# Group softmax: one exponential per tile without the maximum, sums on VectorE, and one test of all sums at the end

## The chip, the core and the metric

The kernel runs on one core of one Trainium2 chip. The core has engines that run beside one another, each with its own list of instructions: VectorE (DVE in the profile), ScalarE (ACT), GpSimd (POOL), TensorE (PE, which this kernel does not use before the change) and SyncE (SP), which issues transfers. They tell one another by semaphores when something is done. Sixteen DMA engines move data between the memory outside (HBM) and the core's own memory (SBUF), in which a tile lies as 128 partitions by some number of elements. A second on-chip memory, PSUM, is used by the changed kernel for small results.

The metric is the device time in microseconds of one execution. Lower is better.

## The reference

```python
def reference(x):                      # x: 4 x 4096 x 4352, float32, normal numbers
    B, N, D = x.shape
    G = 8
    Dg = D // G                        # 544
    x_g = x.reshape(B, N, G, Dg)
    x_g = x_g - x_g.max(axis=-1, keepdims=True)
    exp = np.exp(x_g)
    out = exp / exp.sum(axis=-1, keepdims=True)
    return out.reshape(B, N, D).astype(np.float32)
```

Each row of 4352 numbers is eight groups of 544, and each group gets a softmax of its own. Input and output are 285.21 MB each.

## The kernel before

The 16,384 rows are cut into 64 tiles (`nt`) of 128 partitions with two rows each (`R`), so a tile is 128 x 8704 elements and holds 16 groups per partition (`RG`). There are six buffers (`NT`, `bufs`), and a tile is worked in place in its buffer: tile t lies in buffer t % 6. The order on every engine is written out by hand, with semaphores.

- SP loads the tiles in order (L105). From tile 6 on it first waits until the store of the tile that had the buffer before has landed (`stored`). The last tile is loaded in two halves, one row of each partition at a time (L108), each with a semaphore of its own. Then SP issues the stores of the last two tiles (L113), each behind a wait until that tile is scaled.
- VectorE takes, for each tile, the negated maximum of each group (`vector_max`, L62), and later the reciprocal of the sums (L72) and one multiply of the whole tile by it (L75), both in `vector_scale`. The maximum of the next tile stands ahead of the reciprocal of this one. The list `parts` has 65 entries: 63 whole tiles and the two halves of the last.
- ScalarE takes, for each group, one exponential with the negated maximum as the bias, which also adds up the group's sum (`scalar_exp`, L86): 16 per tile. Its program has a loop around six tiles (L129), and the semaphore `max_done` is counted down once in each turn.
- GpSimd issues the stores of tiles 0 to 61 (L118), each behind a wait until the tile is scaled. At the end it waits until all stores have landed, those of SP too, and then the closing barrier of the block lets the other engines go on (L47).

The steps of the change and of the prediction touch `vector_max`, `scalar_exp` and `vector_scale`, the semaphores between them, and what the engines do after their last part. The loads and the stores, with their queues and their waits, are the same lines in both kernels.

Of the kernel before, what the change touches and what calls it, by code (L numbers as in the profile page):

```python
# [1 line left out]

# [4 lines left out]


@with_exitstack
def kernel(  # L10
    ctx: ExitStack,
    tc: tile.TileContext,
    x: bass.AP,
    out: bass.AP,
):
    nc = tc.nc
    G = 8
    P = 128
    R = 2
    NT = 6  # L20
    RG = R * G
    xf = x.flatten_outer_dims()
    of = out.flatten_outer_dims()
    N, D = xf.shape
    Dg = D // G
    nt = N // (P * R)
    LAST = 2
    FIRST = 2
    turns = (nt - 1 - FIRST) // NT
    f32 = mybir.dt.float32  # L30
    X = mybir.AxisListType.X
    Exp = mybir.ActivationFunctionType.Exp
    xt = xf.rearrange("(t p r) d -> t p (r d)", p=P, r=R)
    ot = of.rearrange("(t p r) d -> t p (r d)", p=P, r=R)

    landed = [tc.alloc_semaphore(f"landed{b}") for b in range(NT)]
    stored = [tc.alloc_semaphore(f"stored{b}") for b in range(NT)]
    last_landed = tc.alloc_semaphore("last_landed")
    last_stored = tc.alloc_semaphore("last_stored")


    max_done = tc.alloc_semaphore("max_done")
    exp_done = tc.alloc_semaphore("exp_done")
    rec_done = tc.alloc_semaphore("rec_done")
    scaled = tc.alloc_semaphore("scaled")

    ctx.enter_context(tc.tile_critical(  # L47
        sync_engine=mybir.EngineType.Pool, no_gpsimd_drain=True))
    bufs = [ctx.enter_context(nc.sbuf_tensor(f"xt{b}", [P, R * D], f32)) for b in range(NT)]
    mx = ctx.enter_context(nc.sbuf_tensor("mx", [P, NT, RG], f32))  # L50
    sm = ctx.enter_context(nc.sbuf_tensor("sm", [P, NT, RG], f32))
    rs = ctx.enter_context(nc.sbuf_tensor("rs", [P, NT, RG], f32))

    parts = [(t, slice(0, RG)) for t in range(nt - 1)]
    parts += [(nt - 1, slice(r * G, (r + 1) * G)) for r in range(R)]

    def groups(t, g):
        return bufs[t % NT][:, :].rearrange("p (g d) -> p g d", d=Dg)[:, g, :]

    def vector_max(n):  # L60
        t, g = parts[n]
        i = nc.vector.reduce_max(  # L62
            out=mx[:, t % NT, g], in_=groups(t, g), axis=X, negate=True)
        if g.start == 0:
            i.wait_op(landed[t % NT], 16 * (t // NT + 1), "sem-ge")
        else:
            i.wait_op(last_landed, 16, "sem-ge")
        i.then_inc(max_done, 1)

    def vector_scale(n):  # L70
        t, g = parts[n]
        nc.vector.reciprocal(out=rs[:, t % NT, g], in_=sm[:, t % NT, g]).wait_op(  # L72
            exp_done, n + 1, "sem-ge").then_inc(rec_done, 1)
        xg = groups(t, g)
        nc.vector.tensor_tensor(  # L75
            out=xg,
            in0=xg,
            in1=rs[:, t % NT, g].unsqueeze(2).to_broadcast([P, g.stop - g.start, Dg]),
            op=mybir.AluOpType.mult,
        ).wait_op(rec_done, n + 1, "sem-ge").then_inc(scaled, 1)  # L80

    def scalar_exp(n, count):
        t, gs = parts[n]
        xg = groups(t, gs)
        for g in range(gs.start, gs.stop):
            i = nc.scalar.activation(  # L86
                out=xg[:, g - gs.start, :],
                in_=xg[:, g - gs.start, :],
                func=Exp,
                bias=mx[:, t % NT, g:g + 1],  # L90
                scale=1.0,
                accum_out=sm[:, t % NT, g:g + 1],
            )
            if g == gs.start:
                i.wait_op(max_done, count, "sem-ge")
        i.then_inc(exp_done, 1)

    for t in range(nt):  # L100
        if t >= NT:
            nc.sync.wait_ge(stored[t % NT], 16 * (t // NT))
        tile_in = bufs[t % NT]
        if t < nt - 1:
            nc.sync.dma_start(out=tile_in[:, :], in_=xt[t]).then_inc(landed[t % NT], 16)  # L105
        else:
            for r in range(R):
                nc.sync.dma_start(  # L108
                    out=tile_in[:, r * D:(r + 1) * D], in_=xt[t, :, r * D:(r + 1) * D],
                ).then_inc(landed[t % NT] if r < R - 1 else last_landed, 16)  # L110
    for t in range(nt - LAST, nt):
        nc.sync.wait_ge(scaled, t + 1 if t < nt - 1 else len(parts))
        nc.sync.dma_start(out=ot[t], in_=bufs[t % NT][:, :]).then_inc(last_stored, 16)  # L113


    for t in range(nt - LAST):
        nc.gpsimd.wait_ge(scaled, t + 1)
        nc.gpsimd.dma_start(out=ot[t], in_=bufs[t % NT][:, :]).then_inc(stored[t % NT], 16)  # L118
    for t in range(nt - NT, nt - LAST):
        nc.gpsimd.wait_ge(stored[t % NT], 16 * (t // NT + 1))  # L120
    nc.gpsimd.drain()
    nc.gpsimd.wait_ge(last_stored, 16 * LAST)

    nc.scalar.preload_act_table(Exp)  # L124

    for n in range(FIRST):
        scalar_exp(n, n + 1)
    nc.scalar.sem_inc(max_done, -FIRST)
    with nc.scalar.Fori(0, turns):  # L129
        for k in range(NT):  # L130
            scalar_exp(FIRST + k, k + 1)
        nc.scalar.sem_inc(max_done, -NT)
    for k, n in enumerate(range(FIRST + turns * NT, len(parts))):
        scalar_exp(n, k + 1)


    vector_max(0)
    for n in range(len(parts)):
        if n + 1 < len(parts):
            vector_max(n + 1)  # L140
        vector_scale(n)


# [1 line left out]
_INS = ['x']  # L145
_OUTS = [((4, 4096, 4352), 'float32')]


# [23 lines left out]
```

## Time and profile before

| what | value |
|---|---|
| median of four runs | 1326.47 us (1326.45 to 1326.55) |
| the profiled execution, its own time | 1327.41 us |
| its span, first to last event of the profile | 1325.6 us |
| VectorE busy | 1190.0 us (90%) |
| ScalarE busy | 757.4 us (57%) |
| GpSimd busy | 33.3 us (3%) |
| moved | 570.48 MB, mean 430 GB/s over the span |
| load of a whole tile, issue to landing, median | 31.1 us |
| store from GpSimd, issue to landing, median | 52.8 us |

An engine's busy time is the sum of its instructions' times, and its share is taken of the span. The span is a little shorter than the execution's own time, since something lies around it. A line of a group names the source line, the engine, the operation, what is written and read with shapes, how often, then the busy time, the mean time of one in ns, and the engine's idle time just ahead of these instructions with what ended most of it. Two of the waits that the trace lists, in all, times and longest: VectorE's maximum waited 110.5 us in 51 waits for loads, and GpSimd's stores waited 1243.2 us in 62 waits for VectorE's multiply.

### The profile page before, as it was taken

The page shows a single profiled execution, that of the slowest core. Times are in us where ns is not written, and L with a number is a line of the kernel's source. Part 1 is how long each engine was busy: PE and PEld are TensorE (multiplying, and loading weights), DVE is VectorE, ACT ScalarE, POOL GpSimd, SP SyncE. Part 2 cuts the span into 40 slices and gives each one's busy share as a digit, 9 for nine tenths or more (in the row PEclk, how much of TensorE's full clock was granted, in tenths as well). Part 3 has the DMA queues.
Part 4 walks back from the last instruction along what each step waited for, and adds up shares of the span by engine and source line. Part 5 has one row for each costly group of instructions (what it writes and reads, how often), then busy time and mean ns, then how long its engine had stood idle before and what let it go on. Part 6 is the DMA issues. An engine that isn't in the chain of part 4 may idle for free.

```text
span 1325.6 us, 2465 instructions
## 1 busy us (share of the span) xinstructions
DVE 1190.0 (90%) x195; ACT 757.4 (57%) x2049; POOL 33.3 (3%) x66
## 2 busy tenths in 40 slices
DVE  5999999998989889899898898988989889898893
ACT  3765566547456465564655646547456474564651
POOL 0000000000000000000000000000000000000000
DMA  9999999999999999999999999999999999999998
GB/s 403 420 436 431 432 433 436 430 435 431 435 436 432 434 430 436 433 434 432 434 435 432 435 430 435 435 434 430 434 436 432 434 431 435 436 431 433 430 438 358
DMA packets 18582, 570.48 MB, mean 430 GB/s; under 512 B 2064, under 2 KB 2064, under 8 KB 2064
## 3 DMA queue, kind: packets, MB, share of 16 engines
q1 hardware_dynamic: 9648, 294.13, 51.5%
q0 software_dynamic: 8928, 276.30, 48.3%
q14 instruction: 6, 0.05, 0.0%
HBM read 285.21 MB, written 285.21 MB: 430 GB/s over the span
## 4 chain that ended last, share of the span: by engine, by line
another core or an unknown queue 69%; DVE 20%; DMA 7%; ACT 1%; SPq 1%; issue 0%; POOLq 0%
DVE xt L75 10%; DVE mx L62 10%; DMA out_dram<-xt 4%; DMA xt<-in_x_dram 3%; ACT xt L86 1%; SPq L105 1%; DVE rs L72 0%; SPq L167 0%; POOLq L47 0%; POOLq L156 0%
## 5 line engine op out<-in xcount | busy, mean ns | idle before, releaser
L86 ACT ACTIVATE xt<-xt,mx 128x544 f32<-128x544 f32 x1024 | 750.1, 734 | 542.2 <-DVE mx L62 542.2
L62 DVE TENSOR_REDUCE mx<-xt 128x16 f32<-128x8704 f32 (+1 forms) x65 | 590.1, 9079 | 110.5 <-DMA xt<-in_x_dram 110.5
L75 DVE TENSOR_TENSOR xt<-xt,rs 128x8704 f32<-128x8704 f32 (+1 forms) x65 | 590.6, 9085 | 2.2
L86 ACT ACTIVATION_READ_ACCUMULATOR xt<-xt,mx 128x1 f32 x1024 | 191.5, 187 | 0.0
L118 POOL DMA_DIRECT2D out_dram<-xt x62 | 33.1, 533 | 1243.2 <-DVE xt L75 1243.2
L72 DVE RECIPROCAL rs<-sm 128x16 f32<-128x16 f32 (+1 forms) x65 | 15.7, 241 | 2.8 <-ACT xt L86 2.8
L124 ACT ACT_TABLE_LOAD x1 | 1.3, 1283 | 0.9 <-PEq L156 0.9
L156 POOL MEMSET const-float32-0.0<- 128x1 f32 x1 | 0.1, 98 | 0.2 <-issue 0.2
L156 POOL MEMSET const-bfloat16-1.0<- 128x1 bf16 x1 | 0.1, 102 | 0.0
L156 POOL MEMSET const-float32-1.0<- 128x1 f32 x1 | 0.1, 98 | 0.0
L156 POOL MEMSET const-uint8-127<- 128x1 uint8 x1 | 0.1, 98 | 0.0
## 6 DMA issues: line engine op xcount, KB each, us to landing
xt<-in_x_dram SPq DMA_DIRECT2D x63, 4352.0 KB, 31.1
out_dram<-xt POOLq DMA_DIRECT2D x62, 4352.0 KB, 52.8
out_dram<-xt SPq DMA_DIRECT2D x2, 4352.0 KB, 21.5
xt<-in_x_dram SPq DMA_DIRECT2D x2, 2176.0 KB, 33.4
```

The lines of the kernel that those rows point to most:

```text
L62: i = nc.vector.reduce_max(out=mx[:, t % NT, g], in_=groups(t, g), axis=X, negate=True)
L72: nc.vector.reciprocal(out=rs[:, t % NT, g], in_=sm[:, t % NT, g]).wait_op(exp_done, n + 1, "sem-ge").then_inc(rec_done, 1)
L75: nc.vector.tensor_tensor(out=xg, in0=xg, in1=rs[:, t % NT, g].unsqueeze(2).to_broadcast([P, g.stop - g.start, Dg]), op=mybir.AluOpType.mu ...
L86: i = nc.scalar.activation(out=xg[:, g - gs.start, :], in_=xg[:, g - gs.start, :], func=Exp, bias=mx[:, t % NT, g:g + 1], scale=1.0, accum ...
L105: nc.sync.dma_start(out=tile_in[:, :], in_=xt[t]).then_inc(landed[t % NT], 16)
L118: nc.gpsimd.dma_start(out=ot[t], in_=bufs[t % NT][:, :]).then_inc(stored[t % NT], 16)
L124: nc.scalar.preload_act_table(Exp)
L156: nc = _bacc.Bacc("TRN2", target_bir_lowering=False, num_devices=1)
```

## The change

Without the subtraction of the maximum, exp(x) / sum(exp(x)) has the same value as long as the sums stay within the range of the numbers. The changed kernel uses that form for every tile. It leaves out `vector_max`; `scalar_exp` is one exponential of a whole part, with no bias and no accumulation, that waits for the load itself; ScalarE's loop is gone. `vector_scale` first takes the sums of the groups with a reduction on VectorE and writes them into PSUM, where the sums of all 64 tiles stay. Reciprocal and multiply are as before, with a wait of the reciprocal for the sums.

After the last multiply, `judge` takes maximum and minimum of all sums, marks those above 1e30 or below 1e-6, adds the marks over the partitions with a matmul of one column of ones, and stores a verdict. SP, ScalarE and VectorE load the verdict into a register and compare it. If it is above 0, they go through a loop over all tiles that computes the softmax with the maximum again, one tile at a time, and stores it over the first result. With the inputs of the reference this loop is not entered.

```diff
@@ -25,11 +25,11 @@
     Dg = D // G
     nt = N // (P * R)
     LAST = 2
-    FIRST = 2
-    turns = (nt - 1 - FIRST) // NT
+    LOW, HIGH = 1e-6, 1e30
     f32 = mybir.dt.float32
     X = mybir.AxisListType.X
     Exp = mybir.ActivationFunctionType.Exp
+    op = mybir.AluOpType
     xt = xf.rearrange("(t p r) d -> t p (r d)", p=P, r=R)
     ot = of.rearrange("(t p r) d -> t p (r d)", p=P, r=R)
 
@@ -37,65 +37,86 @@
     stored = [tc.alloc_semaphore(f"stored{b}") for b in range(NT)]
     last_landed = tc.alloc_semaphore("last_landed")
     last_stored = tc.alloc_semaphore("last_stored")
-
-
-    max_done = tc.alloc_semaphore("max_done")
     exp_done = tc.alloc_semaphore("exp_done")
+    sum_done = tc.alloc_semaphore("sum_done")
     rec_done = tc.alloc_semaphore("rec_done")
     scaled = tc.alloc_semaphore("scaled")
+    tested = tc.alloc_semaphore("tested")
+    counted = tc.alloc_semaphore("counted")
+    judged = tc.alloc_semaphore("judged")
+    again = {k: tc.alloc_semaphore(f"again_{k}") for k in ("in", "max", "exp", "rec", "out", "end")}
 
     ctx.enter_context(tc.tile_critical(
         sync_engine=mybir.EngineType.Pool, no_gpsimd_drain=True))
     bufs = [ctx.enter_context(nc.sbuf_tensor(f"xt{b}", [P, R * D], f32)) for b in range(NT)]
-    mx = ctx.enter_context(nc.sbuf_tensor("mx", [P, NT, RG], f32))
-    sm = ctx.enter_context(nc.sbuf_tensor("sm", [P, NT, RG], f32))
     rs = ctx.enter_context(nc.sbuf_tensor("rs", [P, NT, RG], f32))
+    mx = ctx.enter_context(nc.sbuf_tensor("mx", [P, RG], f32))
+    sm = ctx.enter_context(nc.sbuf_tensor("sm", [P, RG], f32))
+    one = ctx.enter_context(nc.sbuf_tensor("one", [P, 1], f32))
+    extreme = ctx.enter_context(nc.sbuf_tensor("extreme", [P, 4], f32))
+    outside = ctx.enter_context(nc.sbuf_tensor("outside", [P, 4], f32))
+    count = ctx.enter_context(nc.sbuf_tensor("count", [1, 1], f32))
+    verdict = ctx.enter_context(nc.sbuf_tensor("verdict", [1, 1], mybir.dt.int32))
+    half = nt // 2
+    sums = [ctx.enter_context(nc.psum_tensor(f"sums{h}", [P, half, RG], f32)) for h in range(2)]
+    found = ctx.enter_context(nc.psum_tensor("found", [1, 4], f32))
 
     parts = [(t, slice(0, RG)) for t in range(nt - 1)]
     parts += [(nt - 1, slice(r * G, (r + 1) * G)) for r in range(R)]
 
+    def grouped(b):
+        return bufs[b][:, :].rearrange("p (g d) -> p g d", d=Dg)
+
     def groups(t, g):
-        return bufs[t % NT][:, :].rearrange("p (g d) -> p g d", d=Dg)[:, g, :]
-
-    def vector_max(n):
+        return grouped(t % NT)[:, g, :]
+
+    def scalar_exp(n):
         t, g = parts[n]
-        i = nc.vector.reduce_max(
-            out=mx[:, t % NT, g], in_=groups(t, g), axis=X, negate=True)
+        i = nc.scalar.activation(out=groups(t, g), in_=groups(t, g), func=Exp, scale=1.0)
         if g.start == 0:
             i.wait_op(landed[t % NT], 16 * (t // NT + 1), "sem-ge")
         else:
             i.wait_op(last_landed, 16, "sem-ge")
-        i.then_inc(max_done, 1)
+        i.then_inc(exp_done, 1)
 
     def vector_scale(n):
         t, g = parts[n]
-        nc.vector.reciprocal(out=rs[:, t % NT, g], in_=sm[:, t % NT, g]).wait_op(
-            exp_done, n + 1, "sem-ge").then_inc(rec_done, 1)
+        s = sums[t // half][:, t % half, g]
+        nc.vector.reduce_sum(out=s, in_=groups(t, g), axis=X).wait_op(
+            exp_done, n + 1, "sem-ge").then_inc(sum_done, 1)
+        nc.vector.reciprocal(out=rs[:, t % NT, g], in_=s).wait_op(
+            sum_done, n + 1, "sem-ge").then_inc(rec_done, 1)
         xg = groups(t, g)
         nc.vector.tensor_tensor(
             out=xg,
             in0=xg,
             in1=rs[:, t % NT, g].unsqueeze(2).to_broadcast([P, g.stop - g.start, Dg]),
-            op=mybir.AluOpType.mult,
+            op=op.mult,
         ).wait_op(rec_done, n + 1, "sem-ge").then_inc(scaled, 1)
 
-    def scalar_exp(n, count):
-        t, gs = parts[n]
-        xg = groups(t, gs)
-        for g in range(gs.start, gs.stop):
-            i = nc.scalar.activation(
-                out=xg[:, g - gs.start, :],
-                in_=xg[:, g - gs.start, :],
-                func=Exp,
-                bias=mx[:, t % NT, g:g + 1],
-                scale=1.0,
-                accum_out=sm[:, t % NT, g:g + 1],
-            )
-            if g == gs.start:
-                i.wait_op(max_done, count, "sem-ge")
-        i.then_inc(exp_done, 1)
-
-
+    def judge():
+        nc.vector.memset(one[:, :], 1.0).then_inc(tested, 1)
+        flat = [s[:, :, :].rearrange("p t g -> p (t g)") for s in sums]
+        for h in range(2):
+            nc.vector.tensor_reduce(
+                out=extreme[:, h:h + 1], in_=flat[h], axis=X, op=op.max).then_inc(tested, 1)
+            nc.vector.tensor_reduce(
+                out=extreme[:, 2 + h:3 + h], in_=flat[h], axis=X, op=op.min).then_inc(tested, 1)
+        nc.vector.wait_ge(tested, 5)
+        nc.vector.tensor_scalar(
+            out=outside[:, 0:2], in0=extreme[:, 0:2], scalar1=HIGH, scalar2=None,
+            op0=op.is_gt).then_inc(tested, 1)
+        nc.vector.tensor_scalar(
+            out=outside[:, 2:4], in0=extreme[:, 2:4], scalar1=LOW, scalar2=None,
+            op0=op.is_lt).then_inc(tested, 1)
+        nc.tensor.wait_ge(tested, 7)
+        nc.tensor.matmul(
+            out=found[:, :], lhsT=one[:, :], rhs=outside[:, :],
+            start=True, stop=True).then_inc(counted, 1)
+        nc.vector.wait_ge(counted, 1)
+        nc.vector.reduce_sum(out=count[:, :], in_=found[:, :], axis=X).then_inc(tested, 1)
+        nc.vector.wait_ge(tested, 8)
+        nc.vector.tensor_copy(out=verdict[:, :], in_=count[:, :]).then_inc(judged, 1)
 
     for t in range(nt):
         if t >= NT:
@@ -112,7 +133,6 @@
         nc.sync.wait_ge(scaled, t + 1 if t < nt - 1 else len(parts))
         nc.sync.dma_start(out=ot[t], in_=bufs[t % NT][:, :]).then_inc(last_stored, 16)
 
-
     for t in range(nt - LAST):
         nc.gpsimd.wait_ge(scaled, t + 1)
         nc.gpsimd.dma_start(out=ot[t], in_=bufs[t % NT][:, :]).then_inc(stored[t % NT], 16)
@@ -122,23 +142,52 @@
     nc.gpsimd.wait_ge(last_stored, 16 * LAST)
 
     nc.scalar.preload_act_table(Exp)
-
-    for n in range(FIRST):
-        scalar_exp(n, n + 1)
-    nc.scalar.sem_inc(max_done, -FIRST)
-    with nc.scalar.Fori(0, turns):
-        for k in range(NT):
-            scalar_exp(FIRST + k, k + 1)
-        nc.scalar.sem_inc(max_done, -NT)
-    for k, n in enumerate(range(FIRST + turns * NT, len(parts))):
-        scalar_exp(n, k + 1)
-
-
-    vector_max(0)
     for n in range(len(parts)):
-        if n + 1 < len(parts):
-            vector_max(n + 1)
+        scalar_exp(n)
+
+    for n in range(len(parts)):
         vector_scale(n)
+    judge()
+
+    ET = mybir.EngineType
+    regs = nc.alloc_registers("verdict", [ET.SP, ET.Activation, ET.DVE])
+    for e, reg in zip((nc.sync, nc.scalar, nc.vector), regs):
+        e.reg_load(reg, verdict[0:1, 0:1]).wait_op(judged, 1, "sem-ge")
+    with nc.If_cmp(regs, 0, "IS_GT"):
+        for t in range(nt - NT, nt - LAST):
+            nc.sync.wait_ge(stored[t % NT], 16 * (t // NT + 1))
+        nc.sync.wait_ge(last_stored, 16 * LAST)
+        with nc.Fori(0, nt, engines=[ET.SP, ET.Activation, ET.DVE]) as t:
+            nc.sync.dma_start(out=bufs[0][:, :], in_=xt[bass.ds(t, 1)].rearrange("t p f -> (t p) f")).then_inc(
+                again["in"], 16)
+            nc.sync.wait_ge(again["out"], 1)
+            nc.sync.sem_inc(again["out"], -1)
+            nc.sync.dma_start(out=ot[bass.ds(t, 1)].rearrange("t p f -> (t p) f"), in_=bufs[0][:, :]).then_inc(
+                again["end"], 16)
+            nc.sync.wait_ge(again["end"], 16)
+            nc.sync.sem_inc(again["end"], -16)
+
+            nc.scalar.wait_ge(again["max"], 1)
+            nc.scalar.sem_inc(again["max"], -1)
+            for g in range(RG):
+                i = nc.scalar.activation(
+                    out=grouped(0)[:, g, :], in_=grouped(0)[:, g, :], func=Exp,
+                    bias=mx[:, g:g + 1], scale=1.0, accum_out=sm[:, g:g + 1])
+            i.then_inc(again["exp"], 1)
+
+            nc.vector.wait_ge(again["in"], 16)
+            nc.vector.sem_inc(again["in"], -16)
+            nc.vector.reduce_max(
+                out=mx[:, :], in_=grouped(0), axis=X, negate=True).then_inc(again["max"], 1)
+            nc.vector.wait_ge(again["exp"], 1)
+            nc.vector.sem_inc(again["exp"], -1)
+            nc.vector.reciprocal(out=rs[:, 0, :], in_=sm[:, :]).then_inc(again["rec"], 1)
+            nc.vector.wait_ge(again["rec"], 1)
+            nc.vector.sem_inc(again["rec"], -1)
+            nc.vector.tensor_tensor(
+                out=grouped(0), in0=grouped(0),
+                in1=rs[:, 0, :].unsqueeze(2).to_broadcast([P, RG, Dg]),
+                op=op.mult).then_inc(again["out"], 1)
 
 
 # ---- launch: one core; inputs and outputs as the reference has them ----
```

## The prediction, made before the changed kernel ran

> **What bounds the kernel now.** I read the busy shares first, then the chain of waits and SP's own waits, then the end of the span in windows.
>
> ```profile
> DVE 1190.0 (90%) x195; ACT 757.4 (57%) x2049; POOL 33.3 (3%) x66
> ...
> DMA  9999999999999999999999999999999999999998
> ...
> q1 hardware_dynamic: 9648, 294.13, 51.5%
> q0 software_dynamic: 8928, 276.30, 48.3%
> ```
>
> VectorE is busy 90% of the span, but the DMA row is at nine tenths or more in every slice except the last, and the two data queues together fill 99.8% of the span's engine time. So the bytes set the time: one 34,816-byte packet takes 1288 ns in the trace's DMA records in steady state, loads and stores alike, and the packets' time averaged over the 16 DMA engines is 1321.1 us. The first data packet starts at 2.3 us and the last one ends at 1324.2: there is 0.8 us of slack in 1322.
>
> The chain of waits shows the steady state, one load issue after another, 20.6 us apart, each held by a store that frees its buffer (the page can't name the store and calls it unknown; SP's own waits, below, name it):
>
> ```profile
> 1205.61 0.33 SPq L105
> 1205.94 20.27 another core or an unknown queue
> 1226.21 0.02 issue
> 1226.23 30.96 DMA xt<-in_x_dram
> ```
>
> ```profile
> SPq L105 <- DMA out_dram<-xt: 1203.1, 57, 67.6
> SPq L113 <- DVE xt L75: 57.3, 2, 42.1
> SPq L47 <- POOLq L47: 18.7, 1, 18.7
> ```
>
> The last row matters later: after its last store SP has nothing to do for 18.7 us but to wait for GpSimd, which waits for that store to land.
>
> The prices, with shapes kept apart:
>
> ```profile
> L86 ACT ACTIVATE xt<-xt,mx 128x544 f32<-128x544 f32 x1024 | 750.1, 734 | 542.2 <-DVE mx L62 542.2
> L75 DVE TENSOR_TENSOR xt<-xt,rs 128x8704 f32<-128x8704 f32 x63 | 581.2, 9225 | 2.1
> L62 DVE TENSOR_REDUCE mx<-xt 128x16 f32<-128x8704 f32 x63 | 580.8, 9218 | 110.5 <-DMA xt<-in_x_dram 110.5
> L86 ACT ACTIVATION_READ_ACCUMULATOR xt<-xt,mx 128x1 f32 x1024 | 191.5, 187 | 0.0
> L72 DVE RECIPROCAL rs<-sm 128x16 f32<-128x16 f32 x63 | 15.3, 243 | 1.6 <-ACT xt L86 1.6
> L75 DVE TENSOR_TENSOR xt<-xt,rs 128x4352 f32<-128x4352 f32 x2 | 9.4, 4692 | 0.1
> L62 DVE TENSOR_REDUCE mx<-xt 128x8 f32<-128x4352 f32 x2 | 9.4, 4678 | 0.0
> ```
>
> And the end, in windows (busy time of each engine, then clock, DMA share, GB/s):
>
> ```profile
> 1290.00:1300.00 10.00, 9.26 (x3) 5.50 (x15) 0.00 (x0) 1.00 0.99 428
> 1300.00:1310.00 10.00, 4.89 (x2) 0.46 (x2) 0.00 (x0) 1.00 1.01 435
> 1310.00:1320.00 10.00, 0.00 (x0) 0.00 (x0) 0.00 (x0) 1.00 0.97 421
> 1320.00:1326.00 6.00, 0.00 (x0) 0.00 (x0) 0.00 (x0) 1.00 0.05 23
> ```
>
> The DMA share stays near 1 until 1320, although VectorE finishes at 1305.4: even the end is filled with stores.
>
> **The change, part by part.** *Middle, ScalarE.* Sixteen exponentials with accumulation per tile (16 x 0.73 = 11.7 us) become one over 8704 elements. Upper end 11.7 us, if it costs what sixteen do. I take off a start cost, priced by the one-element accumulator read: 16 x (0.734 - 0.187) + 0.187 = 8.9 us, my value; taking it off twice gives 5.9, the lower end. All lie under the 20.6 us that the DMAs need per tile.
>
> *Middle, VectorE.* The maximum goes and a sum of the same shape comes, by the same operation (TENSOR_REDUCE) with another operator and a result in another memory; the two 8704-element rows of this engine differ by 0.007 us, so 9.22 with 0.24 more (a whole reciprocal) as the upper end. The reciprocal now waits for the sum, where before it overlapped the next maximum by 0.08 us. Per tile: 9.22 + 0.03 + 0.24 + 0.03 + 9.22 - 0.08 = 18.66 us, against 18.55 between two multiplies at 53.92 and 72.47 in the timeline. The cover is the DMA period of 20.62: 1.96 us are left, so the edit costs nothing in the middle. Stores go out sooner after a landing (8.9 + 18.7 = 27.6 us, against 39.3 for the tile that landed at 1236.5); that time only moves into the store's queue. GpSimd still issues each store behind its wait, 62 x 0.53 us.
>
> *Start.* The first tile lands at 13.99. Its multiply ends 27.6 us later, at 41.6, against 44.6 now. From then on loads and stores share the engines. So the loads lose half the rate for 3.0 us and get it back at half the rate: every later load lands about 3.0 us later, while the sum of bytes moved stays the same.
>
> *End, worked through.* Tile 62 landed at 1257.2, so now 1260.2; its multiply ends 27.6 us later at 1287.8 (1289.9 before). The halves of the last tile landed at 1272.7 and 1288.2, now 1275.7 and 1291.2. A half's exponential is 8 x 0.547 + 0.187 = 4.6 us, so they are ready at 1280.3 and 1295.8, both ahead of VectorE: two times (4.68 + 0.03 + 0.20 + 0.03 + 4.69) = 19.3 from 1287.8 gives the last store at 1307.1, against 1305.4: 1.7 us later. (Without the shift of the landings: 1304.1.) The exponential's price cancels: what it takes from the chain it adds to the shift. The last store's bytes need 10.3 us (half of 20.6) and the bulk of the DMAs ended at 1321.1; from issue to first packet the first load took 2.3 - 0.9 = 1.4 us. So a last store issued before 1321.1 - 10.3 - 1.4 = 1309.4 finds the engines still at work on the earlier ones and costs nothing: 2.3 us of cover.
>
> *The verdict.* It runs behind VectorE's last multiply, where nothing else is queued. A reduction of 512 elements: the two reduce rows give 1.043 ns an element and 0.14 us fixed, so 0.67 us, four times 2.7. The memset, two tests, the count and the copy by the short reciprocal, 0.20 each, 1.0. One matmul on an idle TensorE has no row: from 0.1 (a memset on GpSimd) to 1.3 (the table load, the longest single small instruction); I take 0.7, nearer to small instructions. Verdict at 1307.1 + 4.4 = 1311.5. The register load on three engines: from 0.33 (SP's DMA issue) to 2 us (a first DMA with its start), I take 1; if it travelled behind the store's packets it would be there at 1324.2. Two jumps over the loop: the trace's six 8 KB instruction transfers take 0.31 to 0.46 us once begun; if a jump had to fetch, it could also wait for one 1.29 us packet on each of two queues: 0 to 3.1 us each, I take 0.5. So all engines stand at the closing barrier at about 1313.5, at 1319.7 by the upper ends. The last store releases them at 1324.4. SP issues its last store ahead of its wait for the verdict, so nothing waits behind that. The cover is the 18.7 us wait of SP, now about 17.
>
> [...]
>
> **The sum.** Profiled execution: span 1325.6 + 0 = 1325.6; what lies around it (1327.4 by its own timing, 1326.47 for the runs shown without a profile) stays. Predicted 1326.5.
>
> **Rivals.** *A: the closing verdict outlasts the last store* (slower). Place: SP, ScalarE and VectorE between the verdict and the barrier. It decides if the load and jumps take over 12.9 us from 1311.5. For it: the queues are full there, and the trace has no register load. Against: the load is no bulk transfer. If it comes behind the store's bytes: 1324.2 plus 0.6 to 6.2 for the jumps, some 1 to 6 us late: about 1330.
>
> *B: VectorE becomes the bound.* From a sum above 20.62 - 9.44 = 11.18 us. At ScalarE's 1.35 ns an element (734 over 544) it would be 11.74: 0.56 x 63 = 35 us, 1362. Against: both rows of VectorE at 1.06 ns.
>
> *C: the DMAs run dry ahead of the last store.* Each microsecond past 1309.4 adds one. If the landings shift by twice my 3.0: 1310.1, 1327.2; beyond 2 us more it would be slower by over 0.2%.
>
> *D: the shorter chain to the last store ends the span earlier* (faster). Place: the last half's exponential, 6.0 us in the chain now, 4.6 then. For it: without the shift the last store leaves 1.3 us earlier. Against: the DMA share until 1320. It can win the 0.8 us of slack, 1325.7, and more only if packets became shorter than 1288 ns.
>
> *E: the general loop is taken.* Sums of 544 exponentials of normal numbers are near 900, far inside 1e-6 to 1e30; 64 tiles one after another would add thousands of us. No chance given.
>
> **How the numbers follow.** Forecast 0.85 (with the small sides of C and D that stay within 0.2%, 2.65 us, about what a measurement of this kernel can tell from no change), A 0.08, C beyond that 0.03, B 0.01, D beyond that 0.03. So faster 0.03, same 0.85, slower 0.12. The forecast's own range is 1325.5 to 1327.5; the unknown load and jumps (A) stretch it upwards, the slack of D and a steadier start downwards: 1324.9 to 1329.5, which leaves out some 1 in 10.
>
> **What would show it.** Right: the DMA row full until about 1320, the exponential near 7 to 9 us, the sum at 9.2, VectorE idle for some 2 us per tile waiting on ScalarE, the last store at about 1307, SP's wait on GpSimd still over 5 us. Wrong: SP or ScalarE arriving last at the barrier (A), a VectorE without waits (B), a gap in the DMA share around 1310 (C), or packets at other than 1288 ns.

## The result and the profile after

The changed kernel takes 1325.16 us (median of 40 runs, 1324.83 to 1325.71) against 1326.48 us (60 runs beside them). The medians differ by 1.3 us; the ratio over all these runs is 0.9988, with an interval of 0.9983 to 0.9992. The profiled execution took 1324.87 us, its span is 1323.1. (Three quarters of the runs of the kernel before lie near 1326.4 and a quarter near 1327.6; its profiled execution was one of the latter.)

The page of the changed kernel, busy times first, then the DMA row, then the queues:

```profile
span 1323.1 us, 475 instructions
...
PE 0.2 (0%) x2; PEld 0.1 (0%) x2; DVE 1199.3 (91%) x204; ACT 478.7 (36%) x66; POOL 33.3 (3%) x66
...
DMA  9999999999999999999999999999999999999999
...
q1 hardware_dynamic: 9648, 294.13, 51.6%
q0 software_dynamic: 8928, 276.30, 48.3%
q14 instruction: 5, 0.04, 0.0%
```

ScalarE has 279 us less work and VectorE 9 more. Both data queues carry the same bytes in the same number of packets, and the DMA row now has a 9 in its last slice as well, where it had an 8. The last line is the DMA traffic that brings instructions to the engines: five packets of 8 KB, one fewer than before.

The groups of instructions, shapes apart (busy us, mean ns of one, idle time ahead and what ended it):

```profile
L85 DVE TENSOR_REDUCE sums<-xt 128x16 f32<-128x8704 f32 x63 | 581.2, 9226 | 104.6 <-ACT xt L75 104.6
L90 DVE TENSOR_TENSOR xt<-xt,rs 128x8704 f32<-128x8704 f32 x63 | 581.1, 9225 | 2.2
L75 ACT ACTIVATE xt<-xt 128x8704 f32<-128x8704 f32 x63 | 469.8, 7457 | 795.5 <-DMA xt<-in_x_dram 795.5
L87 DVE RECIPROCAL rs<-sums 128x16 f32<-128x16 f32 x63 | 16.2, 257 | 2.2
```

The sum costs what the maximum cost (9.23 us). The exponential of a tile takes 7.46 us where sixteen took 11.7, and ScalarE waits for loads most of the time.

SP's waits (us in all, times, longest) and the end of the chain of waits (start, us, what):

```profile
SPq L126 <- DMA out_dram<-xt: 1195.8, 57, 62.4
...
SPq L49 <- POOLq L49: 12.2, 1, 12.2
SPq L155 <- DVE verdict L119: 2.9, 1, 2.9
```

```profile
1260.02 7.46 ACT xt L75
...
1267.50 9.24 DVE sums L85
...
1277.06 9.22 DVE xt L90
1286.28 4.62 DVE sums L85
...
1295.85 4.62 DVE sums L85
...
1300.73 4.69 DVE xt L90
...
1308.57 0.14 DVE verdict L119
```

VectorE's last multiply ends at 1305.4, as before. The verdict is there 3.3 us later. SP waits 2.9 us for it, loads it, passes over the loop, and then still waits 12.2 us for GpSimd, which waits for the last store: the verdict lies wholly beside that store.

So the end of the work on the engines has not moved, and yet the span is shorter. The difference is in the last windows (width, busy time of each engine, clock, DMA share, GB/s). Before:

```profile
1315.00:1320.00 5.00, 0.00 (x0) 0.00 (x0) 0.00 (x0) 1.00 0.93 404
1320.00:1322.00 2.00, 0.00 (x0) 0.00 (x0) 0.00 (x0) 1.00 0.12 52
1322.00:1324.00 2.00, 0.00 (x0) 0.00 (x0) 0.00 (x0) 1.00 0.04 17
```

After:

```profile
1310.00:1315.00 5.00, 0.00 (x0) 0.00 (x0) 0.00 (x0) 0.00 (x0) 0.00 (x0) 1.00 1.01 433
1315.00:1320.00 5.00, 0.00 (x0) 0.00 (x0) 0.00 (x0) 0.00 (x0) 0.00 (x0) 1.00 0.87 376
1320.00:1322.00 2.00, 0.00 (x0) 0.00 (x0) 0.00 (x0) 0.00 (x0) 0.00 (x0) 1.00 0.00 0
```

A window counts a packet where it starts. Before, three packets start between 1320 and 1322 (52 GB/s for 2 us is 104 KB, three times 34,816 bytes) and one more behind 1322: a straggler finishes alone, at 1323.8. After, no packet of that size starts behind 1320, and the last engine is done at 1321.3. Why the last DMA engine comes earlier is the question of the experiments.

The trace has the start and duration of every packet, and the landing of each transfer on each of the 16 DMA engines. From these records, with the first data packet as zero: the engine that is done first and the engine that is done last. "Median" is of the runs, the other columns are of the one profiled execution (us):

| kernel | median | profiled execution | first engine done | last engine done | apart |
|---|---|---|---|---|---|
| before | 1326.48 | 1327.41 | 1317.94 | 1321.86 | 3.9 |
| before, again (e1) | 1326.50 | 1327.83 | 1317.84 | 1322.28 | 4.4 |
| before, third (e14) | 1326.46 | 1326.53 | 1317.82 | 1320.98 | 3.2 |
| after | 1325.16 | 1324.87 | 1317.85 | 1319.32 | 1.5 |
| after, again (e11) | 1325.03 | 1325.22 | 1318.00 | 1319.67 | 1.7 |

The first engine is done at the same time in all five, within 0.2 us. The execution takes 5.55 us more than the last engine's time in each of them. So the bytes take the first engine as long in both kernels, and the whole difference is how far one DMA engine falls behind the others. That distance, the last engine behind the first or behind the median one, is called its lag below.

### The profile page after: what moved, and what is told of

Its sections match the earlier page's. It is cut to its first block, busy times and chain, and to the rows that moved or that the text cites. A ratio compares the mean times of both kernels' runs of the same rounds, so it can differ in the third digit from the quotient of the medians.

```text
span 1323.1 us, 475 instructions
## 1 busy us (share of the span) xinstructions
PE 0.2 (0%) x2; PEld 0.1 (0%) x2; DVE 1199.3 (91%) x204; ACT 478.7 (36%) x66; POOL 33.3 (3%) x66
## 3 DMA queue, kind: packets, MB, share of 16 engines
q1 hardware_dynamic: 9648, 294.13, 51.6%
## 4 chain that ended last, share of the span: by engine, by line
another core or an unknown queue 67%; DVE 21%; DMA 8%; ACT 1%; SPq 1%; issue 0%; PE 0%; POOLq 0%
DVE xt L90 10%; DVE sums L85 10%; DMA xt<-in_x_dram 4%; DMA out_dram<-xt 4%; ACT xt L75 1%; SPq L126 1%; DVE rs L87 0%; DVE extreme L103 0%; DVE extreme L101 0%; PE found L113 0%; DVE outside L106 0%; DVE count L117 0%; DVE verdict L119 0%; DVE outside L109 0%
## 5 line engine op out<-in xcount | busy, mean ns | idle before, releaser
L75 ACT ACTIVATE xt<-xt 128x8704 f32<-128x8704 f32 (+1 forms) x65 | 477.4, 7345 | 815.1 <-DMA xt<-in_x_dram 815.1
L85 DVE TENSOR_REDUCE sums<-xt 128x16 f32<-128x8704 f32 (+1 forms) x65 | 590.6, 9086 | 104.6 <-ACT xt L75 104.6
L87 DVE RECIPROCAL rs<-sums 128x16 f32<-128x16 f32 (+1 forms) x65 | 16.6, 256 | 2.2
L101 DVE TENSOR_REDUCE extreme<-sums 128x1 f32<-128x512 f32 x2 | 1.4, 682 | 0.0
L103 DVE TENSOR_REDUCE extreme<-sums 128x1 f32<-128x512 f32 x2 | 1.4, 678 | 0.0
## 6 DMA issues: line engine op xcount, KB each, us to landing
out_dram<-xt SPq DMA_DIRECT2D x2, 4352.0 KB, 20.6
```

Of the source, the lines that this page charges most:

```text
L75: i = nc.scalar.activation(out=groups(t, g), in_=groups(t, g), func=Exp, scale=1.0)
L85: nc.vector.reduce_sum(out=s, in_=groups(t, g), axis=X).wait_op(exp_done, n + 1, "sem-ge").then_inc(sum_done, 1)
L87: nc.vector.reciprocal(out=rs[:, t % NT, g], in_=s).wait_op(sum_done, n + 1, "sem-ge").then_inc(rec_done, 1)
L101: nc.vector.tensor_reduce(out=extreme[:, h:h + 1], in_=flat[h], axis=X, op=op.max).then_inc(tested, 1)
L103: nc.vector.tensor_reduce(out=extreme[:, 2 + h:3 + h], in_=flat[h], axis=X, op=op.min).then_inc(tested, 1)
```

## The experiments

The runs fall into five groups; each compares with runs of the kernel before on the same chip, whose medians were 1326.48 to 1326.60.

### First group: the verdict, ScalarE's pieces, the time of the stores

**e1**, the kernel before, unchanged.

> The kernel before, unchanged, for a second profile. In the first profiles the landings of 15 of the 16 DMA engines follow one another every 20.57 us per tile in both kernels, while the last engine needs 20.61 with the kernel before and 20.57 with the change: by 1230 us it is some 3 us behind the median. Theory lag (one DMA engine is held up by something the kernel before does all along, and this is the gain): the lag grows again, 2 to 3 us by the end, and the time of this profile is 1326.4 or more. Rival tail (the gain lies ahead of the first or behind the last tile): the lag stays at 1 to 1.3 us in this profile and the median is still 1326.5.

Median 1326.50 (0.9996 [0.9974, 1.0018]); the median repeats, and so does the last engine's lag in the table above.

**e2**, the change without `judge()` and all that follows it.

```diff
-    judge()
-    ET = mybir.EngineType
-    regs = nc.alloc_registers("verdict", [ET.SP, ET.Activation, ET.DVE])
...
```

> The change without the verdict and the general loop (the test of the sums is left out). Forecast of the prediction (the verdict is hidden under the last store): 1325.2, within 0.3 of the change. Rival (the verdict has a price on the path, so the rest of the change gains more than 1.3): under 1324.7. Rival (the verdict or its second set of instructions is itself where the gain comes from): back at 1326.5.

Median 1325.00, 0.9987 [0.9978, 0.9996]. The verdict with its load and its jumps costs 0.2 us at most; the two medians of the change, 1325.16 and 1325.03, differ by nearly as much. One of the twelve executions took 1330.63, and it is the profiled one: its last DMA engine was done at 1325.12, and 5.51 us later the execution ended. The 5.55 us of the table hold for the odd one too, within 0.04.

**e3**, the change with ScalarE's part cut into sixteen again, unrolled, accumulating into memory that nobody reads:

```diff
-        i = nc.scalar.activation(out=groups(t, g), in_=groups(t, g), func=Exp, scale=1.0)
+        for k in range(g.start, g.stop):
+            i = nc.scalar.activation(
+                out=groups(t, g)[:, k - g.start, :], in_=groups(t, g)[:, k - g.start, :],
+                func=Exp, scale=1.0, accum_out=spare[:, t % NT, k:k + 1])
```

> The change with ScalarE's whole-tile exponential cut into 16 of 544 elements with accumulation into a spare tile, all written out (sums still from VectorE; the spare sums are not used). ScalarE has 2,048 records again and some 11.7 us per tile. Theory code (ScalarE's many instructions hold up one DMA engine): 1326.3 to 1327.5, and the last engine's period near 20.61. Theory depth (the time a tile is held between landing and store): hold grows by 4 us only, 1325.2 to 1325.5, period 20.57.

Median 1333.82, 1.0067 [1.0053, 1.008]: 8.7 us worse than the change, though VectorE, order, loads and stores are the same. What stands out on its page is the instruction queue:

```profile
q14 instruction: 20, 0.16, 0.0%
```

Twenty packets where the change has five: ScalarE's 2,048 instructions are written out without a loop, and the trace has reads of 8 KB in between the data packets. The landings show what they do. Each row below is one transfer, a load or a store: the time of its last landing in us, then the landings on the last three of the 16 engines minus the median of the 16, in order; a line says when an 8 KB packet of instructions was read:

```
333.0   0.80  0.91  2.33   load
337.6   instructions read
338.9   0.81  0.96  3.19   store
354.2   0.79  0.98  3.02   load
...
415.8   0.71  1.12  2.94   load
420.6   instructions read
421.8   0.74  1.17  3.80   store
437.1   0.71  1.19  3.65   load
442.2   0.70  1.21  3.61   store
```

With each read one DMA engine falls behind by 0.86 us, of which 0.6 to 0.7 stay; no other one jumps. The work on a tile begins with the last of the sixteen landings: in the change each exponential starts 0.02 us behind it. The lag of the engine that jumps grew from 0.4 us, ahead of the first such read, to 9.6 at about 1180 us. The middle column shows a second thing: the engine next to last creeps, read or no read, by some 0.05 us per tile. Jumping and creeping fall on two different engines.

**e4**, the change with GpSimd's stores issued one part later, to test whether the time for which a buffer is held matters:

```diff
-        nc.gpsimd.wait_ge(scaled, t + 1)
+        nc.gpsimd.wait_ge(scaled, t + 2)
```

> The change with GpSimd's store of tile t issued only when tile t + 1 is scaled too, so a tile is held some 20 us longer (46 us, against 39 in the kernel before and 26 in the change) and the queues of the DMA engines are as shallow as before. Theory depth: 1326.3 to 1327.5. Theory code: 1325.2, last engine's period 20.57.

Median 1332.29, 1.0042 [1.0028, 1.0056], 7.1 us worse than the change. The period of the landings in the steady state is the same (20.567 us at the median engine in both), so a longer hold costs nothing there. The loss is at the start, in windows of this kernel:

```profile
60.00:70.00 10.00, 0.00 (x0) 0.00 (x0) 9.93 (x3) 3.95 (x2) 0.00 (x0) 1.00 0.98 390
70.00:80.00 10.00, 0.00 (x0) 0.00 (x0) 10.00 (x2) 5.93 (x1) 0.53 (x1) 1.00 0.84 331
80.00:90.00 10.00, 0.00 (x0) 0.00 (x0) 9.93 (x3) 0.00 (x0) 0.00 (x0) 1.00 1.01 393
```

The changed kernel moves 446, 446 and 442 GB/s there. All six buffers were full, the sixth at about 68 us, before the first store had freed one, at about 76. The first engine is done 3.5 us later and the lag is 0.8 us larger, so the last engine is 4.3 us later (1323.57 against 1319.32). Another 2.7 us lie behind the last packet (8.2 us instead of 5.55); what they are is open.

### Second group: instructions as such

**e5**, the kernel before with twelve more tiles of ScalarE outside the loop, so that three more blocks of instructions are read:

```diff
-    FIRST = 2
+    FIRST = 14
```

> The kernel before with FIRST = 14: ScalarE's program has 14 tiles written out ahead of its loop in place of 2, so 12 x 32 = 384 instructions more to read and the same instructions executed. Theory blocks (each 8 KB block of instructions that an engine reads holds up one DMA engine by some 0.65 us, as the run with 16 exponentials written out showed, and the kernel before reads more blocks than the change): three blocks more, 1327.8 to 1328.5. Rival (what counts is the number of instructions executed, or the time a tile is held): 1326.5.

Median 1326.69 (1.0001 [0.9992, 1.001]): 0.2 us more, far from three times 0.65. The lag at the end was 3.1 us, as in e14. The landings show why the reads hardly count here. The engine that they push is 2.2 us behind from 350 us on, and stays there; the creeping engine is 0.6 us behind at 390 us, passes it at about 1040, and is the last one at the end (2.75 us behind in the last load).

**e6**, the kernel before without the accumulation, the sums set once to a constant:

```diff
-                accum_out=sm[:, t % NT, g:g + 1],
...
+    nc.vector.memset(sm[:, :, :], 900.0).then_inc(ready, 1)
+    nc.vector.wait_ge(ready, 1)
```

> The kernel before with the accumulation left out of the exponentials (the sums are set to one constant; the output is not normalised): 160 instructions in place of 320 in ScalarE's program, maxima, loop and order as before. Theory blocks: one or two blocks fewer, 1325.2 to 1325.8. Rival depth (a tile is held about as long as before): 1326.3 to 1326.6.

Median 1326.06 (0.9997 [0.9988, 1.0006]), 0.4 us less than before; lag 2.7 us. So the accumulators have a small part in it, and most of the gain is still to be found.

**e7** and **e8**, the change with eight increments of an unused semaphore behind each tile, on ScalarE in e7, on VectorE in e8. They do nothing but lengthen one engine's list; each brings four more packets of instructions (nine in all).

```diff
         scalar_exp(n)
+        for k in range(8):
+            nc.scalar.sem_inc(spare, 1 if k % 2 == 0 else -1)
```

> The change with eight semaphore instructions (plus one, minus one, on a spare semaphore) behind each exponential: 520 instructions more for ScalarE to read, about four blocks, and no work. Theory blocks: 4 x 0.65 = 2.6 us at most, less what another DMA engine is already behind: 1326.2 to 1327.8. Rival (the exponential's form or the shorter hold is the gain): 1325.2 to 1325.4.

> The change with the same eight semaphore instructions behind each multiply on VectorE: 520 more to read, VectorE's own list. Theory blocks with one DMA engine for each list: VectorE's list moves its own DMA engine, 1325.2 to 1327.5 by how far behind that one is. If the blocks of all lists went through one DMA engine: as with ScalarE's padding within 0.3. Rival: 1325.2.

e7: 1326.04, 0.9 us more than the change, lag 2.5 us. e8: 1328.03 (1.0011 [1.0002, 1.002]), 2.9 us more, lag 4.6 us, with the straggler back in the windows of e8:

```profile
1320.00:1322.00 2.00, 0.00 (x0) 0.00 (x0) 0.00 (x0) 0.00 (x0) 0.00 (x0) 1.00 0.16 70
1322.00:1324.00 2.00, 0.00 (x0) 0.00 (x0) 0.00 (x0) 0.00 (x0) 0.00 (x0) 1.00 0.04 17
```

The same four blocks cost 0.7 us each on one list and 0.2 on the other. (In e8 the last engine's lag goes up by 0.8 us at each of the four reads, at 335, 582, 830 and 1057 us, and stays nearly level between them but for 0.2 us at about 720. The engine next to last begins to creep at about 700 us, by 0.06 us per tile.) Why a read costs more on one list than on the other is not shown: the records don't name the DMA engine that it falls on. The change reads five blocks and the kernel before six. By e5 one block of ScalarE's list more or less doesn't give 1.3 us, and e10 below reads six as well and takes the time of the change.

### Third group: how many exponentials

**e9**, the kernel before, order, loop and maxima kept, but one exponential for each part, as in the change (the maximum is taken and not used, so the exponential has no bias to read, and the sums are constant):

```diff
-        for g in range(gs.start, gs.stop):
...
+        i = nc.scalar.activation(out=xg, in_=xg, func=Exp, scale=1.0)
+        i.wait_op(max_done, count, "sem-ge")
```

> The kernel before with maxima, VectorE's order, ScalarE's loop and waits as they were, but one exponential per part in place of sixteen (maximum not subtracted, sums set to one constant: the output is not normalised). Only ScalarE's number of instructions differs from the run without accumulation (1326.06, where one DMA engine fell behind by 0.04 to 0.05 us per tile). Theory activity (the slow drift of one DMA engine comes with ScalarE's many instructions): no drift, 1325.0 to 1325.4. Rival order (it comes with the order and the hold of the kernel before, or its loop): drift as before, 1325.9 to 1326.4.

Median 1325.27, lag 1.8 us: 0.8 us less than e6 and within 0.2 us of the change. (Its ratio in the comparison, 0.9998 [0.9986, 1.0009], carries three executions of the twelve that took 1327 to 1332.)

**e10**, the change with the part in pieces of four groups, four exponentials of 2176 elements per tile.

```diff
-        i = nc.scalar.activation(out=groups(t, g), in_=groups(t, g), func=Exp, scale=1.0)
+        for k in range(g.start, g.stop, 4):
+            i = nc.scalar.activation(
+                out=groups(t, slice(k, k + 4)), in_=groups(t, slice(k, k + 4)), func=Exp, scale=1.0)
```

> The change with ScalarE's exponential in four pieces of 2176 elements: 195 instructions more, one or two 8 KB blocks, and four times the instructions per tile. Theory activity: a drift of a quarter of that with 16 pieces, about 0.01 us per tile or 0.8 us in all, hidden behind the engine that is last anyway or not: 1325.2 to 1326.0. Rival (blocks alone, each 0.65 us on ScalarE's own DMA engine, which in the padded run cost 0.9 for four): 1325.2 to 1325.5 and no drift.

Median 1325.02, lag 1.6 us: four are as good as one.

**e11**, the change again.

> The change, unchanged, for a second profile. Theory lag: no engine falls behind steadily, the last engine's period 20.57 us per tile, its lag at the end under 1.6 us, 1325.1. Rival (the first profile showed a lucky start): a drift of 0.04 or more in this profile, with a time of 1326 or more.

Median 1325.03, 0.9986 [0.9978, 0.9995].

### The last groups: sixteen in a loop

To have sixteen exponentials without the blocks of e3, ScalarE's loop over six tiles is put into the change. TensorE passes the landings on through one semaphore, which ScalarE counts down once in each turn:

```diff
+    for t, g in parts:
+        if g.start == 0:
+            nc.tensor.wait_ge(landed[t % NT], 16 * (t // NT + 1))
...
+        nc.tensor.sem_inc(ready, 1)
...
+    with nc.scalar.Fori(0, turns):
+        for k in range(NT):
+            scalar_exp(FIRST + k, k + 1)
+        nc.scalar.sem_inc(ready, -NT)
```

**e12** has sixteen exponentials per tile in it, **e13** sixteen that also accumulate (`accum_out` into spare memory), **e14** is the kernel before a third time.

> The change with 16 exponentials of 544 elements per tile, no accumulation, in a loop over six tiles as in the kernel before (TensorE passes the landings on through a semaphore that ScalarE counts down each turn). 160 instructions in ScalarE's program, so few blocks to read, but 16 executed per tile. Theory activity (what ScalarE executes makes one DMA engine drift): as the kernel before without accumulation, 1325.9 to 1326.3, drift 0.04 to 0.05 us per tile. Rival order (the drift belongs to the kernel before's order): 1325.0 to 1325.4, drift under 0.02. Rival blocks (only block reads count): 1325.0 to 1325.4.

> The same with accumulation into a spare tile: 320 instructions in ScalarE's program and 32 records per tile, as in the kernel before. Theory activity: 1326.3 to 1326.8. Rival order: 1325.0 to 1325.4. Rival blocks: one or two blocks more than the run without accumulation, within 0.7 above it.

> The kernel before once more, for a profile of one of its usual executions (its times lie at 1326.4, some at 1327.6, and both profiles so far were of the longer kind). Theory lag: in an execution of 1326.4 the last DMA engine is about 1.1 us less behind at the end than in the two profiles (2.5 in place of 3.5 to 4), and the bulk of the engines ends at the same time. Rival: the lag is the same and something else is shorter.

e13 gave 1327.50 (1.0006 [0.9993, 1.0019]), lag 4.2 us: the change with ScalarE's old work is as slow as before, and 1.0 us slower still. e14 gave 1326.46. e12 was a surprise: 1407.83 in the median of six executions, and 1343.01 in the shortest. **e15** is e12 again, and **e16** the same loop with one exponential per part.

> The run with 16 exponentials in the loop, once more: in the first one all DMA engines were slow (loads' packets 1326 ns in the mean against 1291 in the kernel before, times from 1343 to 1411), which no theory here expects. Theory activity: 1325.9 to 1326.6, drift 0.04 to 0.05 us per tile. Rival order: 1325.0 to 1325.4. If the first run was the kernel's own doing: over 1340 again.

> The same loop and the same passing on of landings, with one exponential per tile: the control. Theory activity: 1325.0 to 1325.4 and no drift, as in the change; then neither the loop nor the pass through TensorE moves the time. Rival loop (the drift comes with ScalarE's loop): 1326 or more.

e15: 1405.72 (1342.13 to 1408.84), so it repeats; even the shortest executions are 1.2% above the kernel before. The page of e15 (span, the group of the exponentials, a load queue that has the same bytes):

```profile
span 1406.4 us, 1531 instructions
...
q1 hardware_dynamic: 9648, 294.13, 52.1%
...
L77 ACT ACTIVATE xt<-xt 128x544 f32<-128x544 f32 x1024 | 566.6, 641 | 809.3 <-PEq L152 809.3
```

52.1% of 1406 us is 733 us where the change has 51.6% of 1323, 683 us: the load packets themselves are longer, 1387 ns on average in e15 and 1326 in e12 against 1292 in e16. It isn't all of them: the median packet takes 1288 ns in each, but 16% of e15's load packets take over 1500, and one DMA engine lands its part of a load some 25 us behind the median one from about 340 us on. No other kernel here did that, e13 with the same pieces and an accumulation behind each included. Why is open.

e16: 1325.36 (0.9991 [0.9983, 1.0]); passing the landings on and the loop cost 0.2 to 0.3 us. Its profiled execution was one of the longer ones, 1326.42 with a lag of 2.7 us.

### Where the 1.3 us come from

Two chains of edits start from the two kernels:

| from the kernel before | median us | from the change | median us |
|---|---|---|---|
| before | 1326.48 | after | 1325.03 to 1325.16 |
| without accumulation (e6) | 1326.06 | with landings passed on and loop (e16) | 1325.36 |
| and one exponential per part (e9) | 1325.27 | and sixteen with accumulation (e13) | 1327.50 |

ScalarE's instructions carry 1.2 of the 1.3 us on the left (0.4 for the accumulators, 0.8 for sixteen against one), and 2.1 on the right. The order, the shorter chain and the verdict have 0.1 to 0.2 us left between them. The number of blocks read changes along the chains as well: 6, 4 and 3 on the left, 4 and 7 from e16 to e13. On the left e5 speaks against it. On the right no run separates the two, but e13's landings do: in its loads the engine that a read pushed stays 1.1 us behind, and the creeping one passes it at about 560 us and is 3.1 us behind at the end.

How they act can be seen, not why. From one load of a buffer to the next, taken per tile from 300 to 1225 us, the median engine lands every 20.567 us in all these kernels. The last engine, in the mean of loads and stores:

| kernel | last engine, us per tile |
|---|---|
| before; e1; e14 | 20.611; 20.612; 20.612 |
| e6, no accumulation | 20.600 |
| e13, sixteen with accumulation in the change (20.611 in loads, 20.578 in stores) | 20.595 |
| e16, one exponential in the same loop (a long execution) | 20.595 |
| e9, one exponential in the old order | 20.585 |
| e10, four exponentials | 20.578 |
| after; e11 | 20.571; 20.575 |

The last engine's lag behind the median one, averaged over loads and stores from 250 to 400 us and then from 1100 to 1230, grows by 1.7 to 1.8 us in the three profiles of the kernel before, and by 0.2 and 0.5 in the two of the change. The difference, 1.2 to 1.6 us, is of the size of the gain. In e14 it grows without steps, from the place where the creeping engine has become the last one (about 460 us) to the end; in e11 it jumps at two reads of instructions and stays nearly level between them.

The table says which execution creeps, and that doesn't follow the number of exponentials alone. Leaving e12 and e15 aside, all the profiles with sixteen creep, by 0.04 to 0.06 us per tile once it has begun, and e10 and the two of the change don't. But e9 and e16, with one, creep by 0.03, and e8, with one, by 0.06 from 700 us on. (Where another engine is further behind, as in e5, the table's measure misses it.) So the medians show that ScalarE's edit carries the gain, and the landings that it acts through one late DMA engine; what starts the creeping is not known.

## Why the prediction missed the gain

The time, 1325.16, lies inside the predicted range (1324.9 to 1329.5), but the forecast was no change, and the kernel is faster by more than its measurement leaves in doubt: the interval of the ratio excludes 1, though the 1.3 us are less than the 0.2% that the prediction counted as no change.

**The step that failed** is the first one of the middle: ScalarE's edit was costed at nothing because "All lie under the 20.6 us that the DMAs need per tile". That treats the period as given by the bytes alone and the engines as either late or without effect. By the medians of e6 and e9 ScalarE's instructions cost 1.2 us of the 1.3, and by those of e13 and e16 2.1, though in the kernel before VectorE waits for ScalarE in two places only, 2.8 us in all. What the runs showed in place of the step: in the kernel before one of the 16 DMA engines needs 20.611 us per tile where the others need 20.567, and in the change 20.571 to 20.575. Why ScalarE's instructions have that effect stays open.

**The bound that hid it** is "there is 0.8 us of slack in 1322". It compares the sum of an engine's packet times, 1321.1 us in the mean of the sixteen, with the time from the first packet to the last. But that sum is longer than the time it was meant to fill: the first engine was done 1317.9 us after the first packet and half of them within 1318.7, so packets of one engine must overlap a little, and the difference measures no slack. The last engine was 3.2 to 4.4 us behind the first; an estimate from that is that a kernel whose engines all ended with the first would have saved as much. The prediction's own last window could have shown it: 23 GB/s from 1320 to 1326 are four packets, and it did not ask why they were alone. (On the page's clock the first data packet starts at 1.9 us and the last one ends at 1323.8, both 0.4 less than the prediction has them; only its 1309.4 rests on that, and it takes the sum 1321.1 for a time on the clock besides.)

**Rival D** had the right sign. Its mechanism, a shorter chain to the last store, is not what happened: the last multiply ends at 1305.4 in both. And its condition for more than 0.8 us, packets shorter than 1288 ns, isn't met (the median one takes 1288 ns in both kernels); what changed was how evenly 16 engines ended.

**What held.** The DMA row is full to the end and the first engine's time is the same to 0.2 us, so the bytes do bound the kernel. The sum took 9.23 us (9.22 forecast), and VectorE is idle for 20.57 - 9.23 - 0.26 - 9.23 - 0.06 = 1.8 us per tile (1.96 forecast). A, B, C and E did not come: 12.2 us of cover were left behind the verdict, no sum above 11 us, a DMA share of 1.01 still at 1310 to 1315, and no loop with the maximum among the 475 instructions.

**The exponential** was over-sized: 7.46 us measured against 8.9. The accumulator read (187 ns) was too small a row for the fixed cost that sixteen instructions pay: two sizes of the changed kernel (7.46 us for 8704 elements, 3.83 for 4352) give 0.833 ns an element, so 453 ns for 544, and each of the sixteen took 734. The error was small in effect. But "The exponential's price cancels" was wrong: the first multiply ended 1.7 us ahead of the forecast (39.9 against 41.6), and yet the landing of tile 62 didn't move back by as much; its exponential began at 1260.0 (1260.2 forecast). So the last multiply ended at 1305.4 and not at 1307.1. That it ended where the one of the kernel before did is a coincidence of two shifts.

**The verdict** took 3.3 us (4.4 forecast). The trace has the register loads, 0.78 to 0.87 us on the three engines (1 forecast), and the compare and jump behind each, 0.05 to 0.07: they end at 1309.7, 1.0 us after the verdict (about 2 forecast). It stays beside the last store, and e2 confirms it to 0.2 us. Whether a jump had to fetch, as the forecast's range of 0 to 3.1 us for each allowed, the trace can't decide: one 8 KB read stands at 1313.9, behind the jumps, but all engines wait for the last store until 1321.8, so a wait for it would not show. (The six reads inside the span of the kernel before take 0.31 us each; the 0.46 that the prediction has is of a read ahead of the span.) Reads of instructions did have a price elsewhere: whatever the reading engine itself waits, a DMA engine falls behind by 0.6 to 0.7 us at each read in e3, whose median is 8.7 us above the change's.

## What to carry to other kernels

Compare the first and the last DMA engine at the end before calling the bytes a floor. In the two kernels here the execution ended 5.55 us behind the last of the sixteen, which was 3.2 to 4.4 us behind the first before the change and 1.5 to 1.7 after it, while the DMA row stood at nine tenths or more in every slice but the last one of the kernel before: a mean hides microseconds of lag. Work that hid under the transfers in time still went with a slower DMA engine: by the instructions that were read in, 0.6 to 0.7 us on one DMA engine at each 8 KB read of e3, and with sixteen exponentials per tile on ScalarE, 0.8 us against one by the medians of e6 and e9, which nothing here explains. So few large instructions are worth a try even on an engine with slack. In this kernel one or four pieces in place of sixteen in a loop were worth a tenth of a per cent, and sixteen written out cost 0.7% against one. A loop around sixteen pieces was no sure remedy: 2.3 us over the change in e13, 17 to 86 in e12 and e15.

## What the runs showed that was not expected

- An 8 KB read of instructions put one of the DMA engines 0.6 to 0.7 us behind in e3, with the DMA row at nine tenths or more in every slice but the last (the record of such a read is 0.31 us long in both kernels), and a kernel with 15 more of them and sixteen pieces per tile was 8.7 us slower (e3), where the same pieces in a loop cost 2.3 (e13).
- Eight empty increments per tile, four blocks in all, cost 2.9 us on VectorE's list and 0.9 on ScalarE's (e8, e7).
- One DMA engine creeps behind by some 0.05 us per tile in all profiles with sixteen exponentials per tile on ScalarE, e12 and e15 aside. It doesn't in those of the change and with four, but it does in three others with one (e8, e9, e16). The lines that load and store are the same in all of them. What ties the creeping to ScalarE's work stays open.
- Sixteen exponentials without accumulation, begun as a load lands, stretched the load packets from 1292 to as much as 1387 ns on average, and the kernel took 1342 to 1411 us, twice (e12, e15). No run here tells why.
